# 4-tap convolutions whose running sums stand in the PSUM banks of the scans, with the last tap written to SBUF

## The chip, the cores and the metric

The kernel runs on one core of a Trainium2 chip. The metric is device time in microseconds for one execution. The core has five engines that run at the same time, each through its own list of instructions in order: PE (matrix products), DVE (the vector engine), ACT (the scalar engine, activations), POOL (GpSimd) and SP, which here issues DMAs. They work on SBUF and on PSUM, eight banks of 128 x 512 fp32 that PE writes its products into; DVE and ACT can read and write both. An engine waits where an operand is not there yet, or where the buffer that it is to write is still read.

## The reference, cut to what matters

One layer of a hybrid network over 2048 latent tokens of 1024 values, with 256 context tokens ahead of them. The input projection is split among a Conformer convolution (31 taps), a bidirectional state-space scan (SSD) and a pooling branch; after them come an output projection and a gated MLP with a 3x3 convolution. The change touches the 4-tap convolution ahead of each scan:

```
def _ssd_direction(xbc, dt_raw, conv_w, conv_b, ..., h0, reverse):
    if reverse:
        xbc, dt_raw = xbc[:, ::-1], dt_raw[:, ::-1]
    u = jax.nn.silu(_dwconv1d(xbc, conv_w, conv_b, (SSM_CONV_K - 1, 0)))   # SSM_CONV_K = 4
    xs, Bm, Cm = jnp.split(u, (D_SSM, D_SSM + SSM_GROUPS * SSM_STATE), axis=-1)
    ...
    y, h_final = _ssd_scan(xh, dt, A, Bm, Cm, h0)
```

`xbc` has 1024 channels: 512 of `xs`, 256 of `Bm`, 256 of `Cm`. The convolution runs twice over the same projection with weights of its own, forward in time (direction f) and backward (b). The context runs through the same convolution and scan, without `Cm`, and its last states start the scans of the latent tokens.

## The kernel before, in words

Channels lie on the 128 partitions and tokens along the rows of a tile. The tokens are worked in chunks of 512, of which there are four, 0 to 3. A first sweep runs the context (`ctx_part`), then chunks 0 to 3 forward (`chunk`): projections, both convolutions, the forward scan, the pooling and the 31-tap convolution. A second sweep goes back from chunk 3 with the backward scan and the output projection, and a third part is the MLP. In the profiled execution the first sweep ends at about 716 us.

Every projection (`proj`) of 128 channels by 512 tokens is 24 matmuls: 8 blocks of 128 inputs, each as three products of split values (L114 to L116). It ends in one of four PSUM banks of the pool `mm`. The weights come by DMA from SP (`load_w`), ACT rounds them (L101), POOL subtracts what was rounded off (L102).

In a chunk the eight blocks of `xbc` are projected in the order 4, 5, 6, 7, 0, 1, 2, 3. ACT copies each into a tile `raw` of SBUF (L480; three of them, in turn), with three tokens of the neighbours on either side. `conv4` then forms the forward sum `ca_f` and the backward sum `ca_b`: ACT writes the first tap with the bias (L260), DVE adds three more (L262), ACT applies Silu (L263), forward into `uf` (eight tiles, read by the scan), backward into `ub` (two tiles, sent to DRAM by a DMA and read by the second sweep). The sums stand in three tiles of SBUF, tag `cacc`. They are 512 columns wide forward; backward 509 in chunk 0, 512 in chunks 1 and 2, 515 in chunk 3. In the context both are 256 wide.

The scan works on 128 tokens at a time, in `ssd_in` and `ssd_out`. `ssd_in` forms, in the one bank of the pool `si`, transposes and products (`bps`, `xps`); from there DVE makes `gtm` (L363) and `xde` (L371), and ACT `btm`. `ssd_out` takes three banks in turn from the two of the pool `so`: the state product `st` (L396), which DVE adds to the running state (L399, L402), and the outputs `yo` and `yd`. In the context only `st` is formed, four times: `st_c0_0`, `st_c1_0`, `st_c0_1`, `st_c1_1`, direction first.

In chunk 0 each block is followed by a half of the modulation (`mod_half`): eight weight tiles `wm2` come by DMA and DVE adds them up in a bank `macp` of the pool `lo` (L206, L208), then PE forms `modp` (L211). The pooling sum `pr` (L667) and the 31-tap convolution `c31p` (L585, L588) run on DVE too; `c31p` keeps its sum in a PSUM bank of `lo`, and its last tap goes to SBUF. `dt_path` (L269 and on) computes the step sizes.

The order of the instructions is not that of the code: a scheduler simulates a timeline and lays out each engine's list from it. PSUM and SBUF tiles come from pools that hand out buffers in turn, so a new tile waits until the last reader of the tile that had its buffer is done.

Of the kernel before, what the change touches and what calls it, by code (L numbers as in the profile page):

```python
# [7 lines left out]
F32 = mybir.dt.float32  # L8
F32R = mybir.dt.float32r
AL = mybir.AluOpType  # L10
AF = mybir.ActivationFunctionType
PSUM = bass.MemoryType.PSUM

P = 128
# [34 lines left out]
class Kern:  # L49
# [201 lines left out]

    def conv4(self, out, raw, lo, n, d, j, name):
        nc = self.nc
        acc = self.pc.tile([P, 515], F32, tag="cacc", name=f"ca_{name}", bufs=3)
        base = COFF["sc_w"] + (d * 8 + j) * 4
        for k in range(4):
            off = lo + (k if d == 0 else 3 - k)
            wk = self.cols[:, base + k : base + k + 1]
            if k == 0:
                nc.scalar.activation(acc[:, :n], raw[:, off : off + n], AF.Identity, bias=self.col("sc_b", d * 8 + j), scale=wk)  # L260
            else:
                nc.vector.scalar_tensor_tensor(acc[:, :n], raw[:, off : off + n], wk, acc[:, :n], AL.mult, AL.add)  # L262
        nc.scalar.activation(out, acc[:, :n], AF.Silu)  # L263

    def dt_path(self, hs, n, key, name):
        nc, sp = self.nc, self.sp
# [195 lines left out]
    def chunk(self, c):  # L462
        nc, t, p1 = self.nc, self.t, self.p1
        n = CH
        last = c == NCH - 1
        hs = self.make_h(lambda k: t["xT"][k, :, c * CH : (c + 1) * CH], n, 0, f"c{c}")
        rows = self.dt_path(hs, n, c, f"c{c}")
        for d in range(2):
            nc.sync.dma_start(self.s[f"arow{c}"][d].rearrange("s h l -> (s h) l"), rows[:, d, :])
        self.glu(c, hs)  # L470
        hal = None if last else p1.tile([P, 8, 3], F32, tag="hal", name=f"hal{c}")
        uf = [None] * 8
        for qi, j in enumerate((4, 5, 6, 7, 0, 1, 2, 3)):
            ps = self.proj(self.load_w(t["w_x"][j], f"x{c}_{j}"), hs, n, f"x{c}_{j}")
            raw = self.pc.tile([P, 518], F32, tag="raw", name=f"raw{c}_{j}", bufs=3)
            if c == 0:
                nc.gpsimd.memset(raw[:, 0:3], 0.0)
            else:
                nc.gpsimd.tensor_copy(raw[:, 0:3], self.hal[:, j, :])
            nc.scalar.activation(raw[:, 3:515], ps, AF.Copy)  # L480
            if last:
                nc.gpsimd.memset(raw[:, 515:518], 0.0)
            else:
                nc.gpsimd.tensor_copy(hal[:, j, :], raw[:, 512:515])
            f = self.sp.tile([P, 512], F32, tag="uf", name=f"uf{c}_{j}", bufs=8)
            self.conv4(f, raw, 0, n, 0, j, f"f{c}_{j}")
            uf[j] = f
            b = self.pc.tile([P, 515], F32, tag="ubc", name=f"ub{c}_{j}", bufs=2)
            i0 = 3 if c == 0 else 0
            m = 515 - i0 if last else 512 - i0  # L490
            self.conv4(b[:, :m], raw, i0, m, 1, j, f"b{c}_{j}")
            t0 = c * CH - 3 + i0
            nc.sync.dma_start(self.s["ub"][j, :, t0 : t0 + m], b[:, :m])
            if c == 0:
                self.mod_half(qi)
        self.hal = hal

        def fwd(s):
            nm = f"f{c}_{s}"
            ins[s] = self.ssd_in(0, c, s, uf, s * P, True, nm)  # L500

        def out(s):
            y = self.ssd_out(0, c, s, ins[s], f"f{c}_{s}")
            nc.sync.dma_start(self.s[f"yf{c}"][s * P : (s + 1) * P, :], y)

        ins = {}
        self.ppool(c, hs)
        for s in range(SB - 1):
            fwd(s)
        if not last:  # L510
            self.zproj(c, hs)
        for s in range(NSUB):
            out(s)
            if s + SB - 1 < NSUB:
                fwd(s + SB - 1)
        self.pool_branch(c)
        self.conv_branch(c)
        if last:
            self.zproj(c, hs)
# [538 lines left out]
```

## Time and profile before

| what | value |
|---|---|
| median of 3 runs | 2626.35 us (2623.07 to 2632.42) |
| profiled execution, its own time | 2625.29 us |
| its span, first to last instruction | 2623.6 us |
| mean granted clock of PE | 0.953 |
| busy: PE, DVE, ACT, POOL | 2419.6, 1840.7, 1145.5, 1336.3 us |

Names in the profile are the program's, without their numbers: `ca_f` stands for the forward sums of all chunks, `ps_z` for a projection into `zt`, and so on. A row of a group gives the line, the engine, the operation, what is written and what is read, the count, then the busy time and the mean of one instruction in ns, then how long the engine stood idle just ahead of them and what ended most of it. A row of the timeline gives the start in us, the duration, the instruction, and in brackets how long the engine waited ahead of it and for whom. In the table of stretches stand the borders and the length, then per engine the busy time and the count, then the granted clock, the busy share of the DMA engines and the GB/s that they moved. A row of waits gives the waiting instruction and the one that it waited for, the sum of the waits, their count, the longest.

### The profile page before, as it was taken

What the parts mean: (1) busy time and instruction counts of PE and PEld (TensorE: products, weight loads), DVE (VectorE), ACT (ScalarE), POOL (GpSimd) and SP (SyncE); (2) the same over time, 40 slices, a digit from 0 to 9 for tenths busy, and PEclk for the clock granted to TensorE, in tenths of its full rate; (3) what the DMA queues carried; (4) which work ended last, traced back from release to release, by engine and by line L of the source; (5) the groups of instructions that cost most, each with busy time, mean ns of one, the idle gap of its engine ahead of it and who ended that gap; (6) DMA issues with size and microseconds to landing.
All of it is one profiled execution on the core that took longest, in us unless ns stands there. A gap on an engine that the chain in (4) does not pass through costs nothing.

```text
span 2623.6 us, 31624 instructions
## 1 busy us (share of the span) xinstructions
PE 2419.6 (92%) x11338; PEld 1996.2 (76%) x11338; DVE 1840.7 (70%) x2681; ACT 1145.5 (44%) x1761; POOL 1336.3 (51%) x928
## 2 busy tenths in 40 slices
PE   6897999898777988899999999999999999999996
PEld 3776777677665766689998878888878888788885
DVE  5898978689965776577555497665696664876655
ACT  2656565756553334433334333344333344233342
POOL 2555565554533554544446455455454464454444
PEclk7998999999867999899999999999999999999998
DMA  7655343343335565662224343333343343433332
GB/s 286 202 152 164 110 135 121 117 125 106 123 126 189 185 213 182 194 218 89 89 89 127 100 139 105 96 116 112 114 135 96 97 121 97 152 97 103 99 97 73
DMA packets 125838, 347.01 MB, mean 132 GB/s; under 512 B 19680, under 2 KB 24176, under 8 KB 125680
## 3 DMA queue, kind: packets, MB, share of 16 engines
q1 hardware_dynamic: 121072, 336.60, 40.5%
q10 hardware_dynamic: 4608, 8.39, 1.0%
q8 instruction: 89, 1.46, 0.2%
q14 instruction: 69, 0.57, 0.1%
HBM read 298.63 MB, written 46.31 MB: 131 GB/s over the span
## 4 chain that ended last, share of the span: by engine, by line
PE 59%; DVE 21%; DMA 6%; ACT 6%; issue 4%; POOL 3%; SPq 0%; ACTq 0%; POOLq 0%; DVEq 0%
PE d L114 6%; PE d L116 6%; PE d L115 6%; PE ug L114 5%; PE ug L115 5%; PE ug L116 5%; PE uv L114 5%; PE uv L115 5%; PE uv L116 5%; DVE ca_f L262 2%; DVE ca_b L262 2%; DVE fa L882 1%; DVE c31p L588 1%; ACT E_f L351 1%; DMA wm<-in_w_mod 1%
## 5 line engine op out<-in xcount | busy, mean ns | idle before, releaser
L882 DVE SCALAR_TENSOR_TENSOR fa<-gbuf,cols,fa 128x512 f32<-128x512 f32 x704 | 523.7, 754 | 224.4 <-ACT fa L878 201.8
L912 DVE TENSOR_TENSOR gl<-g,gh 128x512 fp32r<-128x512 f32 x176 | 197.2, 1131 | 217.6 <-ACT gh L911 196.5
L102 POOL TENSOR_TENSOR wl_d<-wr_d,wh_d 128x1024 fp32r<-128x1024 f32 x88 | 222.1, 2525 | 210.6 <-ACT wh_d L101 210.6
L102 POOL TENSOR_TENSOR wl_uv<-wr_uv,wh_uv 128x1024 fp32r<-128x1024 f32 x88 | 220.4, 2504 | 205.9 <-ACT wh_uv L101 205.9
L114 PE MATMUL ug<-h2h,wh_ug 128*128 128x512 f32 (+3 forms) x880 | 309.3, 351 | 17.2 <-DVE g L890 10.6
L102 POOL TENSOR_TENSOR wl_ug<-wr_ug,wh_ug 128x1024 fp32r<-128x1024 f32 x88 | 214.4, 2436 | 192.3 <-ACT wh_ug L101 192.3
L115 PE MATMUL ug<-h2l,wh_ug 128*128 128x512 f32 (+3 forms) x880 | 308.7, 351 | 0.0
L116 PE MATMUL ug<-h2h,wl_ug 128*128 128x512 f32 (+3 forms) x880 | 308.2, 350 | 0.0
L114 PE MATMUL uv<-h2h,wh_uv 128*128 128x512 f32 x704 | 275.6, 391 | 8.8 <-DVE g L890 8.5
L115 PE MATMUL uv<-h2l,wh_uv 128*128 128x512 f32 x704 | 275.3, 391 | 0.0
L116 PE MATMUL uv<-h2h,wl_uv 128*128 128x512 f32 x704 | 274.9, 390 | 0.0
L114 PE MATMUL d<-wh_d,gh 128*128 128x512 f32 x704 | 274.0, 389 | 0.6 <-ACT fg L884 0.4
L115 PE MATMUL d<-wl_d,gh 128*128 128x512 f32 x704 | 273.9, 389 | 0.0
L116 PE MATMUL d<-wh_d,gl 128*128 128x512 f32 x704 | 263.7, 389 | 0.0
L911 ACT ACTIVATE gh<-g 128x512 fp32r<-128x512 f32 x176 | 110.8, 630 | 247.8 <-PE d L115 225.9
L114 PEld LDWEIGHTS ug<-h2h,wh_ug 128*128 128x128 f32 x880 | 168.3, 191 | 37.6 <-DVE g L890 11.9
L101 ACT ACTIVATE wh_ug<-wr_ug 128x1024 fp32r<-128x1024 f32 x88 | 93.2, 1059 | 221.3 <-PE uv L115 188.4
L115 PEld LDWEIGHTS ug<-h2l,wh_ug 128*128 128x128 f32 x880 | 168.2, 191 | 17.8
L116 PEld LDWEIGHTS ug<-h2h,wl_ug 128*128 128x128 f32 x880 | 168.4, 191 | 16.7
L588 DVE SCALAR_TENSOR_TENSOR c31p<-gl,cols,c31p 128x512 f32<-128x512 f32 x232 | 162.1, 749 | 13.6 <-ACT c31p L585 13.4
L114 PEld LDWEIGHTS uv<-h2h,wh_uv 128*128 128x128 f32 x704 | 132.9, 189 | 36.7 <-DVE g L890 9.2
L101 ACT ACTIVATE wh_uv<-wr_uv 128x1024 fp32r<-128x1024 f32 x88 | 93.2, 1059 | 145.5 <-PE ug L115 89.8
(388 smaller groups left out, 5585.5 us busy)
## 6 DMA issues: line engine op xcount, KB each, us to landing
wr_ug<-in_w_up SPq DMA_DIRECT2D x88, 512.0 KB, 3.6
wr_uv<-in_w_up SPq DMA_DIRECT2D x88, 512.0 KB, 3.6
wr_d<-in_w_dn SPq DMA_DIRECT2D x88, 512.0 KB, 3.5
wm<-in_w_mod SPq DMA_DIRECT2D x64, 256.0 KB, 4.0
wr_x<-in_w_x SPq DMA_DIRECT2D x32, 512.0 KB, 3.8
wr_o<-in_w_o SPq DMA_DIRECT2D x32, 512.0 KB, 4.2
wm<-in_w_mod SPq DMA_DIRECT2D x16, 512.0 KB, 8.1
x_c<-in_xT SPq DMA_DIRECT2D x32, 256.0 KB, 3.4
```

Of the source, the lines that this page charges most:

```text
L101: nc.scalar.activation(hi, src, AF.Copy)
L102: nc.gpsimd.tensor_tensor(lo, src, hi.bitcast(F32), AL.subtract)
L114: nc.tensor.matmul(out, a[0], b[0], start=first, stop=False)
L115: nc.tensor.matmul(out, a[0], b[1], start=False, stop=False)
L116: nc.tensor.matmul(out, a[1], b[0], start=False, stop=last)
L262: nc.vector.scalar_tensor_tensor(acc[:, :n], raw[:, off : off + n], wk, acc[:, :n], AL.mult, AL.add)
L351: nc.scalar.activation(E[:, h, :], E[:, h, :], AF.Relu, bias=cum[:, d, s, h : h + 1], scale=-1.0)
L588: nc.vector.scalar_tensor_tensor(to[:, :m], gl[:, j, o + k : o + k + m], w[k], acc[:, :m], AL.mult, AL.add)
L882: nc.vector.scalar_tensor_tensor(acc, G[:, dr : dr + 8, dc : dc + GW], wc[i], acc, AL.mult, AL.add)
L911: nc.scalar.activation(gh, gt[k], AF.Copy)
L912: nc.vector.tensor_tensor(gl, gt[k], gh.bitcast(F32), AL.subtract)
```

## The change

`conv4` takes its running sum from a bank of the pool `so` where the sum has at most 512 columns: all of the context, all forward sums, and the backward sums of chunks 0 to 2. The backward sums of chunk 3, of 515 columns, stay in SBUF, where there are now two tiles `cacc` for three. For all sums the third of DVE's taps no longer goes back into the sum but into `uf` or `ub`, and Silu runs in place there. Silu's line is L267 in the changed kernel, the taps L266, the first tap L263, and later lines move by four.

```
     def conv4(self, out, raw, lo, n, d, j, name):
         nc = self.nc
-        acc = self.pc.tile([P, 515], F32, tag="cacc", name=f"ca_{name}", bufs=3)
+        if n <= 512:
+            acc = self.bank(self.so, f"ca_{name}")
+        else:
+            acc = self.pc.tile([P, 515], F32, tag="cacc", name=f"ca_{name}", bufs=2)
         base = COFF["sc_w"] + (d * 8 + j) * 4
         for k in range(4):
             off = lo + (k if d == 0 else 3 - k)
...
             if k == 0:
                 nc.scalar.activation(acc[:, :n], raw[:, off : off + n], AF.Identity, bias=self.col("sc_b", d * 8 + j), scale=wk)
             else:
-                nc.vector.scalar_tensor_tensor(acc[:, :n], raw[:, off : off + n], wk, acc[:, :n], AL.mult, AL.add)
-        nc.scalar.activation(out, acc[:, :n], AF.Silu)
+                to = out if k == 3 else acc[:, :n]
+                nc.vector.scalar_tensor_tensor(to, raw[:, off : off + n], wk, acc[:, :n], AL.mult, AL.add)
+        nc.scalar.activation(out, out, AF.Silu)
...
-            self.conv4(f, raw, 0, n, 0, j, f"f{c}_{j}")
+            self.conv4(f[:, :n], raw, 0, n, 0, j, f"f{c}_{j}")
```

The scheduler lays out new lists with it. Up to the middle of the second sweep they differ, and from there on the last 7309 rows of PE, 905 of DVE, 824 of ACT, 546 of POOL and 424 of SP stand in the same order as before.

In the rows below a tile's name ends in a number of its own, and x2 or x4 counts equal rows. The first place is DVE where chunk 0's convolutions begin. Before, `state_c0_0`, the first copy of a context state, was followed by the taps of block 4, and the operands `xde` of the other three states came between taps:

```order
L208 SCALAR_TENSOR_TENSOR macc4_1410<-wm2_4_7_1432,scol_138,macp4_1409 128x512
L399 COPY state_c0_0_707<-st_c0_0_704 128x512
L262 SCALAR_TENSOR_TENSOR ca_f0_4_1067<-raw0_4_1062,cols_105,ca_f0_4_1067 128x512
L262 SCALAR_TENSOR_TENSOR ca_b0_4_1074<-raw0_4_1062,cols_105,ca_b0_4_1074 128x509
L262 SCALAR_TENSOR_TENSOR ca_f0_4_1067<-raw0_4_1062,cols_105,ca_f0_4_1067 128x512
L262 SCALAR_TENSOR_TENSOR ca_b0_4_1074<-raw0_4_1062,cols_105,ca_b0_4_1074 128x509
L262 SCALAR_TENSOR_TENSOR ca_f0_4_1067<-raw0_4_1062,cols_105,ca_f0_4_1067 128x512
L371 TENSOR_TENSOR xde_c1_0_719<-xps_c1_0_714,ex_ctx_686 128x512
L262 SCALAR_TENSOR_TENSOR ca_b0_4_1074<-raw0_4_1062,cols_105,ca_b0_4_1074 128x509
```

Now all four states' operands stand ahead of the first tap, and the last addition, `state_c1_1`, ahead of the first backward tap:

```order
L403 COPY state_c0_0_707<-st_c0_0_704 128x512
L375 TENSOR_TENSOR xde_c1_0_719<-xps_c1_0_714,ex_ctx_686 128x512
L403 COPY state_c1_0_724<-st_c1_0_721 128x512
L375 TENSOR_TENSOR xde_c0_1_736<-xps_c0_1_731,ex_ctx_686 128x512
L406 TENSOR_TENSOR state_c0_1_741<-state_c0_1_741,st_c0_1_738 128x512
L375 TENSOR_TENSOR xde_c1_1_754<-xps_c1_1_749,ex_ctx_686 128x512
L266 SCALAR_TENSOR_TENSOR ca_f0_4_1067<-raw0_4_1062,cols_105,ca_f0_4_1067 128x512 x2
L212 TENSOR_TENSOR modc2_115<-modp5_1517,cols_105 128x4
L266 SCALAR_TENSOR_TENSOR uf0_4_1066<-raw0_4_1062,cols_105,ca_f0_4_1067 128x512
...
L208 SCALAR_TENSOR_TENSOR macp6_1573<-wm2_6_1_1578,scol_138,macp6_1573 128x512
L406 TENSOR_TENSOR state_c1_1_759<-state_c1_1_759,st_c1_1_756 128x512
L266 SCALAR_TENSOR_TENSOR ca_b0_4_1074<-raw0_4_1062,cols_105,ca_b0_4_1074 128x509
```

So the first forward tap moved behind `xde_c1_1`, and the backward taps of the same block, which alternated with it, behind the end of the context's scan.

The second place is PE at the fourth context state. Before, the matmul `st_c1_1` and the transposes `dtT` of chunk 0 stood between the whole projections of blocks 2 and 3:

```order
L114 MATMUL ps_x0_2_1529<-hhi_c0_7_813,wh_x0_2_1524 128x512
L115 MATMUL ps_x0_2_1529<-hlo_c0_7_814,wh_x0_2_1524 128x512
L116 MATMUL ps_x0_2_1529<-hhi_c0_7_813,wl_x0_2_1525 128x512
L396 MATMUL st_c1_1_756<-xde_c1_1_754,btm_c1_1_747 128x256 x2
L275 MATMUL dtT_c0_845<-ident_107,dtr_c0_843 128x40 x4
L114 MATMUL ps_x0_3_1611<-hhi_c0_0_764,wh_x0_3_1606 128x512
L115 MATMUL ps_x0_3_1611<-hlo_c0_0_765,wh_x0_3_1606 128x512
L116 MATMUL ps_x0_3_1611<-hhi_c0_0_764,wl_x0_3_1607 128x512
```

Now they stand in the projection of block 2, behind its first three matmuls:

```order
L116 MATMUL ps_x0_1_1447<-hhi_c0_7_813,wl_x0_1_1443 128x512
L211 MATMUL modp5_1517<-ones_122,macc5_1492 128x2 x4
L114 MATMUL ps_x0_2_1529<-hhi_c0_0_764,wh_x0_2_1524 128x512
L115 MATMUL ps_x0_2_1529<-hlo_c0_0_765,wh_x0_2_1524 128x512
L116 MATMUL ps_x0_2_1529<-hhi_c0_0_764,wl_x0_2_1525 128x512
L400 MATMUL st_c1_1_756<-xde_c1_1_754,btm_c1_1_747 128x256 x2
L279 MATMUL dtT_c0_845<-ident_107,dtr_c0_843 128x40 x4
L114 MATMUL ps_x0_2_1529<-hhi_c0_1_771,wh_x0_2_1524 128x512
L115 MATMUL ps_x0_2_1529<-hlo_c0_1_772,wh_x0_2_1524 128x512
L116 MATMUL ps_x0_2_1529<-hhi_c0_1_771,wl_x0_2_1525 128x512
```

The state matmul moved forward by the 21 other matmuls of that projection.

The third place is ACT where the raw tiles of chunk 0's first blocks are filled and emptied (`wh` rows are weights that ACT rounds). Before, `raw0_7` was copied behind Silu of the second block's backward sum, `ub0_5`:

```order
L480 ACTIVATE raw0_6_1226<-ps_x0_6_1201 128x512
L260 ACTIVATE ca_f0_6_1231<-raw0_6_1226,cols_105 128x512
L260 ACTIVATE ca_b0_6_1238<-raw0_6_1226,cols_105 128x509
L263 ACTIVATE ub0_5_1155<-ca_b0_5_1156 128x509
L101 ACTIVATE wh_x0_2_1524<-wr_x0_2_1523 128x1024
L480 ACTIVATE raw0_7_1308<-ps_x0_7_1283 128x512
L263 ACTIVATE ub0_6_1237<-ca_b0_6_1238 128x509
```

Now it stands behind the first tap of that sum, `ca_b0_5`, whose bank `ca_b0_4` has to leave first:

```order
L267 ACTIVATE uf0_4_1066<-uf0_4_1066 128x512
L263 ACTIVATE ca_b0_4_1074<-raw0_4_1062,cols_105 128x509
L263 ACTIVATE ca_f0_5_1149<-raw0_5_1144,cols_105 128x512
L293 ACTIVATE dt_e_c0_851<-dt_x_c0_850 128x64
L294 ACT_TABLE_LOAD
L294 ACTIVATE dt_e_c0_851<-dt_e_c0_851 128x64
L101 ACTIVATE wh_p0_1_1720<-wr_p0_1_1719 128x1024
L267 ACT_TABLE_LOAD
L267 ACTIVATE ub0_4_1073<-ub0_4_1073 128x509
L263 ACTIVATE ca_b0_5_1156<-raw0_5_1144,cols_105 128x509
L484 ACTIVATE raw0_7_1308<-ps_x0_7_1283 128x512
L267 ACTIVATE uf0_5_1148<-uf0_5_1148 128x512
```

The Silus of block 5 and the first taps of block 6, which stood ahead of it, now come behind it, and the loads of activation tables (`ACT_TABLE_LOAD`) fall between other rows; there are 49 of them in the whole program where there were 45.

## The prediction

> **What bounds the kernel now.** I read the page first: the busy line of each engine, the slices of the span, the chain of work that ended last. Then the stretches of the first third, because only there the changed lines run, then what PE waited for in them, and last single rows on DVE and POOL where PE waited longest.
>
> ```profile
> PE 2419.6 (92%) x11338; PEld 1996.2 (76%) x11338; DVE 1840.7 (70%) x2681; ACT 1145.5 (44%) x1761; POOL 1336.3 (51%) x928
> PE 59%; DVE 21%; DMA 6%; ACT 6%; issue 4%; POOL 3%; SPq 0%; ACTq 0%; POOLq 0%; DVEq 0%
> ...
> L262 DVE SCALAR_TENSOR_TENSOR ca_f<-raw,cols,ca_f x96: 644/745/2900, 130.1 to 669.6; 128x512 f32<-128x512 f32 x96
> ```
>
> PE is the bound of the program as a whole. The taps of the 4-tap convolutions, L262, are done before 680 us, and behind the first sweep, which ends at about 716 us, nothing of the changed code runs; there I forecast no difference. So the question is how much PE idles in the first 716 us, and for whom. In these stretches (borders at the starts of the chunks' convolutions) the columns are the stretch and its length, then busy time and count for PE, PEld, DVE, ACT, POOL, and the granted clock:
>
> ```profile
> 90.00:230.00 140.00, 122.98 (x547) 97.47 (x545) 122.47 (x185) 80.94 (x129) 71.79 (x55) 0.93 0.54 170
> 230.00:291.00 61.00, 55.73 (x280) 44.70 (x281) 54.04 (x84) 36.32 (x61) 33.76 (x24) 0.97 0.46 139
> 291.00:442.00 151.00, 140.63 (x654) 110.76 (x653) 122.54 (x189) 96.68 (x155) 87.46 (x66) 0.97 0.39 126
> 442.00:601.00 159.00, 143.07 (x681) 113.31 (x679) 127.91 (x199) 95.90 (x156) 86.65 (x67) 0.98 0.39 118
> 601.00:716.00 115.00, 97.25 (x422) 75.84 (x421) 112.33 (x199) 68.19 (x117) 60.30 (x39) 0.91 0.34 113
> ```
>
> PE idles 17.0, 5.3, 10.4, 15.9 and 17.8 us in them. Up to 601 us it is PE's own work with DVE a close second (77 to 89% busy); from 601 to 716 us DVE is busy 112.33 of 115 us, so the end of the sweep hangs on DVE.
>
> **What the taps cost.** A tap that keeps its sum in SBUF takes 745 ns at the median, yet its mean is far higher. Taps of the 31-tap convolution, L588, of the same shape, keep their sum in PSUM:
>
> ```profile
> L588 DVE SCALAR_TENSOR_TENSOR c31p<-gl,cols,c31p 128x512 f32<-128x512 f32 x232 | 162.1, 749 | 13.6 <-ACT c31p L585 13.4
> L262 DVE SCALAR_TENSOR_TENSOR ca_f<-raw,cols,ca_f 128x512 f32<-128x512 f32 x96 | 96.7, 1008 | 31.1 <-ACT ca_f L260 30.8
> L262 DVE SCALAR_TENSOR_TENSOR ca_b<-raw,cols,ca_b 128x512 f32<-128x512 f32 x48 | 43.0, 896 | 0.1
> L262 DVE SCALAR_TENSOR_TENSOR ca_b<-raw,cols,ca_b 128x509 f32<-128x509 f32 x24 | 28.3, 1178 | 0.0
> L262 DVE SCALAR_TENSOR_TENSOR ca_b<-raw,cols,ca_b 128x515 f32<-128x515 f32 x24 | 22.8, 950 | 2.2 <-ACT ca_b L260 2.1
> ...
> L588 DVE SCALAR_TENSOR_TENSOR c31p<-gl,cols,c31p x232: 733/749/760, 217.3 to 740.0; 128x512 f32<-128x512 f32 x116
> L588 DVE SCALAR_TENSOR_TENSOR c<-gl,cols,c31p x8: 734/738/748, 288.4 to 740.8; 128x512 f32<-128x512 f32 x8
> ...
> 508.41 2.88 DVE L262 SCALAR_TENSOR_TENSOR ca_f<-raw,cols,ca_f 128x512 f32<-128x512 f32 x1
> ...
> 507.93 2.81 POOL L102 TENSOR_TENSOR wl_z<-wr_z,wh_z 128x1024 fp32r<-128x1024 f32 x1 [1.39 <-ACT wh_z L101]
> ```
>
> The last two rows show one long tap: it begins 0.48 us into a POOL subtraction and ends 0.55 us behind its end. None of the 232 PSUM taps exceeds 760 ns, though POOL works half of the time. So I take it that only the tap with both inputs in SBUF waits for POOL. The last tap of the 31-tap convolution reads SBUF and PSUM and writes SBUF, as the new last tap does, and takes 738 ns: no wait either.
>
> **The change, part by part.** DVE: 72 + 24 + 24 + 24 = 168 taps of chunks 0 to 3 in direction f and chunks 0 to 2 in b go to PSUM (x96 of ca_f, x48 and x24 of ca_b); the 24 of 515 columns stay in SBUF. Saved: 96 x (1008 - 749) + 48 x (896 - 749) + 24 x (1178 - 749) = 24.9 + 7.1 + 10.3 = 42 us of DVE's time, and some 8 us more on 36 taps of the context, before 108 us, where input DMAs and the modulation set the pace; those I count at nothing. Of the 42 us most lies beside PE's work. By stretch (DVE's busy time and count first; ca_f and ca_b apart in chunk 0, L262 as a whole in chunks 1 and 2, ca_f alone in chunk 3; a PSUM tap's own share, with the overlap of rows taken off, is 162.1 / 232 = 0.70 us):
>
> ```profile
> 90.00:230.00 140.00, 23.01 (x24) 11.32 (x16) 0.93 0.54 170
> 90.00:230.00 140.00, 28.27 (x24) 11.17 (x16) 0.93 0.54 170
> 291.00:442.00 151.00, 47.43 (x49) 0.97 0.39 126
> 442.00:601.00 159.00, 41.47 (x48) 0.98 0.39 118
> 601.00:716.00 115.00, 23.56 (x24) 10.41 (x15) 0.91 0.34 113
> ```
>
> Above 0.70 us a tap this is 17.7 us in chunk 0, 13 in chunk 1, 8 in chunk 2 and 6.8 (f alone) in chunk 3. What of it PE waited for between 230 and 601 us:
>
> ```profile
> PE xps_f L369 <- DVE gtm_f L363: 10.9, 3, 7.5
> ...
> 518.08 1.11 PE L369 MATMUL xps_f<-ident,uf 128*128 128x128 f32 x4 [7.54 <-DVE gtm_f L363]
> 518.84 0.77 PE L116 MATMUL ps_z<-hhi_c,wl_z 128*128 128x512 f32 x1
> ...
> 522.36 0.39 PE L115 MATMUL ps_z<-hlo_c,wh_z 128*128 128x512 f32 x1
> ...
> 526.94 0.39 PE L114 MATMUL ps_z<-hhi_c,wh_z 128*128 128x512 f32 x1
> ```
>
> (a) Chunks 1 and 2. `gtm_f` stands on DVE right behind a chunk's convolutions and holds the bank that PE wants; 7.5 us in chunk 2 and, of the other 3.4 us (10.9 - 7.5), 2.6 us in chunk 1 are the convolutions' lateness. It will not all go: ahead of `gtm_f` stand two `pr` rows of the pooling that wait for POOL,
>
> ```profile
> 512.65 0.73 DVE L667 SCALAR_TENSOR_TENSOR pr<-ps,cols,pb 64x512 f32<-64x512 f32 x1
> 514.63 2.93 DVE L667 SCALAR_TENSOR_TENSOR pr<-ps,cols,pb 64x512 f32<-64x512 f32 x1 [1.24 <-POOL ps L646]
> ```
>
> and POOL itself was late, since its subtraction waits for ACT, whose Silu waits for the taps. I take 6 of the 7.5 us as gone, plus 1.7 us of slow matmuls behind the gap (8 steps of 0.44 us from 518.84 to 522.36, then 20 of 0.23 us: 8 x 0.21), and chunk 1's 2.6 us with 0.4 us of the same: 8 + 3 = 11 us. Bounds: 0, if `pr` alone sets `gtm_f`; 17 us, if the 15 us of both rows go, with 2 us of slow matmuls.
>
> (b) Chunk 3 and the end of the sweep. DVE is the limit there, so DVE time saved is time saved: 6 us (the 6.8 above, less rows that wait for other engines). Bounds 2, if half the lateness returns as waits for ACT, and 10, the 6.8 and DVE's own 2.7 us of idling.
>
> (c) Chunk 0. The two PSUM banks are those of the scans, in turn. The context's four state matmuls come between its convolutions and chunk 0's, so the first tap, at 130.1 us before, must now wait for the third state, and the backward one for the fourth (159.5 and 176.2 us before):
>
> ```profile
> 130.12 0.75 DVE L262 SCALAR_TENSOR_TENSOR ca_f<-raw,cols,ca_f 128x512 f32<-128x512 f32 x1 [2.40 <-ACT ca_f L260]
> 159.53 0.67 DVE L402 TENSOR_TENSOR state_c<-state_c,st_c 128x512 f32<-128x512 f32 x1
> 176.23 0.68 DVE L402 TENSOR_TENSOR state_c<-state_c,st_c 128x512 f32<-128x512 f32 x1
> 168.29 2.07 PE L396 MATMUL st_c<-xde_c,btm_c 128*128 128x256 f32 x4 [2.98 <-DVE xde_c L371]
> 203.53 0.98 PE L211 MATMUL modp<-ones,macc 128*128 128x2 f32 x4 [4.95 <-DVE macc L208]
> 207.26 0.64 PE L314 MATMUL cum_c<-dt_a_c,tri 128*128 128x32 f32 x2 [2.75 <-DVE dt_a_c L309]
> ```
>
> The new order draws the fourth state matmul 21 matmuls forward (5 us at 0.23 us) and takes its operand's row, which PE awaited for 3.0 us, ahead of the taps; so I set the last state at 176 - 5 - 3 = 168 us at the latest, and at about 161 us if PE runs there without the waits it had from 138 us on. From 161 us: ACT's first tap 0.8, the three backward taps of j = 4 with six rows of other work between them, 9 x 0.75 = 6.8, then ACT's Silu, next first tap and copy, 2.0 us: at about 171 us a raw tile and a PSUM bank come free for PE's projection of x3. It ran from about 171 us before too, behind the state matmul of 168.29 us and four transposes. Further on DVE owes 17.7 us less of locks and one modulation half less (8 rows of some 0.75 us, 6 us, drawn ahead of the taps), against the 26 us from 130 to 156 us in which it has no tap. So PE's 4.95 and 2.75 us at 203 to 207 us may shrink, and new waits for raw tiles may come (three tiles, each held until its backward sum is written). I take 0; bounds: -8 us, both waits gone, and +22 us, worked out with rival 2.
>
> (d) The rest:
>
> ```profile
> L263 ACT ACT_TABLE_LOAD x13 | 16.7, 1283 | 0.2
> L263 ACT ACTIVATE ub<-ca_b 128x512 f32<-128x512 f32 x16 | 10.0, 627 | 7.8 <-DVE ca_b L262 7.7
> L260 ACT ACTIVATE ca_f<-raw,cols 128x512 f32<-128x512 f32 x32 | 25.9, 809 | 0.8
> L585 ACT ACTIVATE c31p<-gl,cols 128x512 f32<-128x512 f32 x8 | 6.0, 772 | 0.0
> 139.28 1.54 DVE L262 SCALAR_TENSOR_TENSOR ca_f<-raw,cols,ca_f 128x512 f32<-128x512 f32 x2 [0.21 <-ACT ca_f L260]
> ```
>
> The last tap now waits on DVE for the tile that it writes, where Silu waited on ACT; Silu's waits were all for taps, none for a DMA that empties the tile, so I price this at nothing. If the cover went, each late DMA would stop DVE, and with it ACT's next first tap. ACT's first tap takes 772 ns into PSUM for 809 ns: 56 x 0.04 = 2 us on ACT, hidden beside DVE's taps. Two taps of one sum behind each other take 1.54 us, 0.1 us more than two of 0.70 us; the new order has 9 more such pairs, 1 us of DVE, hidden in (b)'s rounding. The new order has 49 table loads on ACT for 45, two more in chunk 0 and two in chunk 3: 4 x 1.3 = 5 us, for which I charge nothing, since ACT works 81 of 140 us in the one and 68 of 115 us in the other; without that cover each would hold a Silu, and behind it the taps of a later sum, by 1.3 us, so chunk 3's 2.6 us are within (b)'s lower bound. Silu runs in place on SBUF as it read SBUF before; the third SBUF sum buffer goes, and only chunk 3's backward sums use the two that are left.
>
> Sum: -11 - 6 + 0 = -17 us. The profiled execution took 2625.3 us (span 2623.6), 1.1 us under the median of 2626.35. So 2608 us on its scale, 2609 us for the median.
>
> [...]
>
> **Rivals.** (1) The taps were hidden anyway: PE is 92% busy, `pr` and POOL keep `gtm_f` late, and only the end of the sweep gains. For it speaks POOL's wait row above; against it that POOL itself hung on the taps by way of ACT. Time: 2626 - 6 = 2620 us. (2) Slower: chunk 0's late convolutions. If the fourth state stays at 176 us, chunk 0's pairs of convolutions start 46 us later than 130.1 us; less 17.7 us of locks and 6 us of modulation done ahead, DVE is 22 us late, and PE, with three raw tiles and four banks, loses as much. With (a) and (b) that is 2626 + 22 - 17 = 2631 us, with (b) alone 2642 us; I set it at 2636 us. It decides from a fourth state at about 170 us on, where the 24 us of relief no longer cover the delay. Against it speaks that PE's order has that matmul three rows into the projection of x2, which began 24 rows ahead of 168.29 us. (3) Larger gain: chunk 0 also loses its 8 us of waits, and (a) comes near its bound: 2626 - 30 = 2596 us.
>
> **Numbers.** Forecast 0.55, rival 1 0.23, rival 2 0.14, rival 3 0.08. A difference of 0.3% is 7.9 us. Faster than 2618.5 us are the forecast but for a small part, and rival 3: 0.62. Rival 1 and a rest are within 0.3%: 0.23. Slower 0.15. The range leaves out most of rival 2 and the far half of rival 3: 2596 to 2630 us; the forecast's own is 2600 to 2618 us.
>
> **What would show it.** No tap in PSUM above 760 ns, group means near 749 ns, and long rows only among the 515-column ones. PE's wait for `gtm_f` in chunk 2 below 2 us. The last forward state matmul of the sweep about 17 us earlier, the stretch from 811 us on as long as before. The fourth context state at about 161 us, the projection x3 of chunk 0 starting at about 171 us. Wrong it would be if DVE's saved time turns into waits for ACT, whose first tap now needs a bank that the tap two sums earlier must have left, or if chunk 0's PE waits exceed 15 us.

## The result, and the profile after

The changed kernel takes 2609.3 us (median of 4 runs, 2605.0 to 2611.4), the kernel before, run beside it, 2624.9 us. The ratio is 0.9934, 95% interval 0.9918 to 0.9951: 0.66% faster, 16 us. The forecast was 2609 us. The total came out as forecast; two of the terms of its sum did not, and they cancelled, which was luck.

The profiled execution took 2605.0 us, 4.3 us under its median; its span is 2603.3 us, 20.3 us shorter than that of before. The busy line of the page:

```profile
PE 2403.8 (92%) x11338; PEld 1987.1 (76%) x11338; DVE 1791.9 (69%) x2681; ACT 1149.7 (44%) x1765; POOL 1303.9 (50%) x928
```

DVE is busy 49 us less, where the working had 42 us and 8 us of the context. The taps, one row for each form, with minimum, median and maximum in ns and the starts of the first and the last:

```profile
L266 DVE SCALAR_TENSOR_TENSOR ca_f<-raw,cols,ca_f x64: 734/748/756, 154.9 to 649.0; 128x512 f32<-128x512 f32 x64
L266 DVE SCALAR_TENSOR_TENSOR ca_b<-raw,cols,ca_b x64: 734/748/2045, 162.0 to 651.0; 128x512 f32<-128x512 f32 x32, 128x509 f32<-128x509 f32 x16, 128x515 f32<-128x515 f32 x16
L266 DVE SCALAR_TENSOR_TENSOR uf<-raw,cols,ca_f x32: 644/736/748, 158.0 to 653.0; 128x512 f32<-128x512 f32 x32
L266 DVE SCALAR_TENSOR_TENSOR ub<-raw,cols,ca_b x32: 720/742/755, 166.2 to 655.8; 128x512 f32<-128x512 f32 x16, 128x509 f32<-128x509 f32 x8, 128x515 f32<-128x515 f32 x8
```

The forward taps, all in PSUM, reach 756 ns at most, where the same rows in SBUF reached 2900 ns. Only the backward group still has long ones (up to 2045 ns); it holds the sums of 515 columns, which stayed in SBUF.

Where the time went is read from the start of the same matmul, counted by its name, in the traces. The points are the first projection into a raw tile of chunks 1, 2 and 3, the last forward state matmul `st_f`, the first matmul of the output projection `o`, the first of the MLP `ug` and the last of all, `d`. E1 is the first experiment below.

| start in us | chunk 1 | chunk 2 | chunk 3 | last st_f | first o | first ug | last d |
|---|---|---|---|---|---|---|---|
| before | 280.5 | 433.8 | 584.6 | 727.2 | 811.0 | 1116.0 | 2602.2 |
| after | 272.4 | 420.4 | 563.4 | 705.5 | 785.9 | 1095.8 | 2581.9 |
| after less before | -8.1 | -13.4 | -21.2 | -21.7 | -25.1 | -20.2 | -20.3 |
| E1 less before | +1.5 | +5.2 | +4.3 | +5.9 | -0.8 | +6.4 | +5.8 |

So context and chunk 0 gave 8.1 us, chunks 1 and 2 together 13.1, chunk 3 with the end of the sweep 0.5. Behind it 3.4 us were won up to the output projection, 4.9 lost up to the MLP, and nothing changed in the MLP. Two cautions go with such a table. Each column is one execution: that of E5 below, whose lists are the changed kernel's until well into chunk 3, reaches chunk 3 2.8 us later, so differences of up to 3 us say little. And the lists differ in how many of PE's matmuls stand ahead of chunk 1's first projection, 1056 before and 1050 after; behind 1056 matmuls the changed kernel leads by 6.7 us, and chunks 1 and 2 then give 14.5. From chunk 2 on the counts are equal.

The stretches, with the columns of the same table of before and the same borders, though the changed kernel's work lies up to 22 us earlier in them:

```profile
90.00:230.00 140.00, 123.23 (x559) 96.96 (x558) 96.22 (x182) 87.95 (x136) 66.74 (x59) 0.94 0.54 172
230.00:291.00 61.00, 60.11 (x307) 48.44 (x306) 54.87 (x86) 33.23 (x60) 34.45 (x27) 0.99 0.45 140
291.00:442.00 151.00, 142.14 (x689) 114.50 (x688) 121.69 (x215) 102.00 (x164) 80.67 (x68) 0.99 0.41 130
442.00:601.00 159.00, 150.04 (x708) 119.11 (x707) 128.99 (x226) 100.38 (x161) 82.93 (x68) 0.99 0.39 121
601.00:716.00 115.00, 89.44 (x388) 70.09 (x386) 105.56 (x171) 65.05 (x114) 50.40 (x36) 0.84 0.41 130
```

From 90 to 230 us DVE is 26 us less busy, and PE's idle time hardly moves (16.8 us for 17.0), though more matmuls are done there (559 for 547). From 230 to 601 us PE idles 18.7 us where it idled 31.6.

### The profile page after: what moved, and what is told of

Read it like the earlier page. It is cut to its first block, busy times and chain, and to the rows that moved or that the text cites. A ratio compares the mean times of both kernels' runs of the same rounds, so it can differ in the third digit from the quotient of the medians.

```text
span 2603.3 us, 31634 instructions
## 1 busy us (share of the span) xinstructions
PE 2403.8 (92%) x11338; PEld 1987.1 (76%) x11338; DVE 1791.9 (69%) x2681; ACT 1149.7 (44%) x1765; POOL 1303.9 (50%) x928
## 4 chain that ended last, share of the span: by engine, by line
PE 61%; DVE 20%; DMA 6%; ACT 6%; issue 3%; POOL 2%; SPq 0%; ACTq 0%; DVEq 0%; POOLq 0%
PE d L114 6%; PE d L116 6%; PE d L115 6%; PE ug L114 5%; PE ug L115 5%; PE ug L116 5%; PE uv L114 5%; PE uv L115 5%; PE uv L116 5%; DVE c31p L592 2%; DVE fa L886 1%; DVE xt L783 1%; ACT E_f L355 1%; DMA x_c<-in_xT 1%; PE o L114 1%
## 5 line engine op out<-in xcount | busy, mean ns | idle before, releaser
L116 PEld LDWEIGHTS ug<-h2h,wl_ug 128*128 128x128 f32 x880 | 168.6, 192 | 16.8
L592 DVE SCALAR_TENSOR_TENSOR c31p<-gl,cols,c31p 128x512 f32<-128x512 f32 x232 | 162.2, 746 | 20.3 <-ACT c31p L589 20.0
```

Source lines behind the costliest of these rows:

```text
L116: nc.tensor.matmul(out, a[1], b[0], start=False, stop=last)
L592: nc.vector.scalar_tensor_tensor(to[:, :m], gl[:, j, o + k : o + k + m], w[k], acc[:, :m], AL.mult, AL.add)
```

## The experiments

Theory: taps with both inputs in SBUF waited for POOL's subtraction, and the PSUM sums only take these waits away. Rivals: the new order of the lists brought the gain, or the last tap's place did. Several kernels are held to the order of another: the program is built twice, and the second build's instructions get order-only edges along the first one's lists, engine by engine (shortened, as are the other cuts of code):

```
first = build_one(arrays, "psum")               # the kernel whose order is wanted
...
for n in first.order:                           # n: place of an instruction in the code
    i = mine[n]
    if i.engine in last:
        tc.add_manual_dep(i, last[i.engine].name, NoSync, ...)
    last[i.engine] = i
```

**E1: the changed kernel's order, sums in SBUF.**

```
-        if n <= 512:
+        if n <= 512 and self.mode == "psum":
             acc = self.bank(self.so, f"ca_{name}")
         else:
-            acc = self.pc.tile([P, 515], F32, tag="cacc", name=f"ca_{name}", bufs=2)
+            w, tag = (512, "cacf") if n <= 512 else (515, "cacc")
+            acc = self.pc.tile([P, w], F32, tag=tag, name=f"ca_{name}", bufs=2)
```

> The changed kernel with every engine's list in exactly the changed kernel's order, but the running sums in two SBUF tiles of their own in place of the two PSUM banks; the last tap still goes to uf or ub, Silu is still in place. Theory (waits for POOL): the taps' mean goes back from 745 ns to 950 ns or more, DVE's busy time before 716 us grows by about 40 us, and the time goes back to within 6 us of the kernel before, that is 10 to 20 us above the changed kernel. Rival (the new order or the last tap's place brought the gain): the taps are long again, but the time stays within 4 us of the changed kernel.

Measured: 2630.3 us, ratio to before 1.0010 (0.9998 to 1.0023), span 2629.3 us. The groups of its taps:

```profile
L267 DVE SCALAR_TENSOR_TENSOR ca_f<-raw,cols,ca_f 128x512 f32<-128x512 f32 x64 | 59.8, 934 | 19.6 <-ACT ca_f L264 19.4
L267 DVE SCALAR_TENSOR_TENSOR ca_b<-raw,cols,ca_b 128x512 f32<-128x512 f32 (+2 forms) x64 | 57.2, 894 | 8.0 <-ACT ca_b L264 7.7
L267 DVE SCALAR_TENSOR_TENSOR uf<-raw,cols,ca_f 128x512 f32<-128x512 f32 x32 | 37.9, 1183 | 0.2
L267 DVE SCALAR_TENSOR_TENSOR ub<-raw,cols,ca_b 128x512 f32<-128x512 f32 (+2 forms) x32 | 30.0, 938 | 0.2
```

The theory holds and the first rival falls: with every list in the same order the whole gain is gone. This splits the change in two. At one order the faster taps are worth 21 us by the medians (2630.3 to 2609.3) and 26 us by the two spans (2629.3 to 2603.3); the changed kernel's profiled execution was the fastest of its four. The new order with sums in SBUF is 5.8 us behind the kernel before in the table, but its ratio to it has 1 within the interval, so a cost of the order by itself is not shown.

**E2: DVE's first tap reads SBUF twice and writes the bank.**

```
+            one = self.pc.tile([P, 512], F32, tag="cacf", ...)     # ACT's first tap goes here
...
-    nc.vector.scalar_tensor_tensor(to, raw[...], wk, acc[:, :n], AL.mult, AL.add)
+    nc.vector.scalar_tensor_tensor(to, raw[...], wk, (one if k == 1 else acc)[:, :n], AL.mult, AL.add)
```

> The changed kernel, same order on every engine, but ACT's first tap goes to an SBUF tile, so DVE's first tap reads two SBUF tiles and writes the PSUM bank; the other two are as in the changed kernel. Theory (a tap waits for POOL when both inputs are in SBUF, wherever it writes): a third of the 168 taps is long again, mean of that third above 0.95 us with single ones above 2.5 us, the other two thirds stay below 760 ns, and the time rises by a third of what the sums in SBUF cost, 3 to 7 us above the changed kernel. Rival (only a tap that also writes SBUF waits): no tap above 760 ns and the time as the changed kernel's within 3 us.

Measured: 2613.5 us, ratio 0.9946 (0.9928 to 0.9965), 4.2 us above the changed kernel's median, with intervals that overlap; it is the rows that decide. Forward taps by form, those that read `cs_f` in SBUF first:

```profile
L267 DVE SCALAR_TENSOR_TENSOR ca_f<-raw,cols,cs_f x32: 740/755/1808, 155.1 to 650.5; 128x512 f32<-128x512 f32 x32
L267 DVE SCALAR_TENSOR_TENSOR ca_f<-raw,cols,ca_f x32: 736/750/756, 155.9 to 653.7; 128x512 f32<-128x512 f32 x32
L267 DVE SCALAR_TENSOR_TENSOR uf<-raw,cols,ca_f x32: 649/739/750, 158.1 to 657.7; 128x512 f32<-128x512 f32 x32
```

Two inputs in SBUF make a tap long although it writes PSUM (up to 1808 ns); with one input in PSUM it is not (756 ns at most), although it writes SBUF (`uf`, 750 ns at most). The size was off: the means of the first taps in the chunks are 820 ns forward and 842 ns backward, not above 950, and none exceeds 2.1 us.

**E3: the kernel before, its own order, without POOL's subtraction in the first sweep.** POOL fills the low halves of these weights with zeros instead, so this kernel leaves them out of its products.

```
-        self.split(w, hi, lo)
+        if self.mode == "fill" and name[0] in "xcgapz":  # weights of the context and the chunks
+            self.nc.scalar.activation(hi, w, AF.Copy)
+            self.nc.gpsimd.memset(lo.bitcast(F32), 0.0)
+        else:
+            self.split(w, hi, lo)
```

> The kernel before, every engine's list in its own order, but POOL's subtraction for the weights of the context and of the four chunks is a memset of the same tile (the low halves of these weights are left out of the products). Theory (POOL's two-input subtraction is what the SBUF taps wait for): the mean of the SBUF taps falls from 980 to 1008 ns to below 800 ns without any PSUM sum, DVE's busy time before 716 us falls by 30 us or more, and the time falls by 8 to 20 us. Rival (the taps are slow for another reason, their own SBUF traffic or the DMAs'): the taps stay above 950 ns and the time within 4 us of the kernel before. If a memset holds DVE as well, long taps stay, but as long as a memset's rest.

Measured: 2551.4 us, ratio 0.9712 (0.9697 to 0.9726). The groups, then one tap on DVE's timeline and the memset on POOL's that it lies in:

```profile
L266 DVE SCALAR_TENSOR_TENSOR ca_b<-raw,cols,ca_b 128x512 f32<-128x512 f32 (+2 forms) x96 | 74.7, 778 | 2.4 <-ACT ca_b L264 2.1
L266 DVE SCALAR_TENSOR_TENSOR ca_f<-raw,cols,ca_f 128x512 f32<-128x512 f32 x96 | 73.8, 769 | 44.7 <-ACT ca_f L264 42.1 <-POOL hal L488 2.3
```

```profile
142.36 0.75 DVE L266 SCALAR_TENSOR_TENSOR ca_b<-raw,cols,ca_b 128x509 f32<-128x509 f32 x1
141.95 0.95 POOL L111 MEMSET wl_x<- 128x1024 f32 x1 [3.13 <-PE ps_x L120]
```

The SBUF taps fall to 769 and 778 ns without any sum in PSUM, and a memset does not hold the tap that starts within it (0.75 us). So POOL's two-input subtraction is the cause of the long taps. The gain of 76 us is far above the 8 to 20 us expected: the taps are one of several groups of DVE that this subtraction holds (the twelve `pr` rows of 512 columns fall from 927 to 744 ns on average; of the 85 us by which DVE's busy time falls, 1840.7 to 1755.8 us, the taps of the chunks give 42), and POOL itself needs 0.95 us for 2.6 us. How much of it is whose was not separated.

**E4: the last tap back in the bank, Silu reads the bank.** `to = acc[:, :n]` for all taps, and `activation(out, acc[:, :n], AF.Silu)`.

> The changed kernel, same order on every engine, but the last tap goes back into the PSUM bank and Silu reads the bank and writes uf or ub. Theory (the banks alone carry the gain): last taps of 749 ns for 737 ns, 56 x 12 ns = 0.7 us of DVE, Silu a little slower, the time within 3 us of the changed kernel. Rival (the last tap's place matters, since it frees a bank one ACT instruction earlier): the banks come free 0.6 us or more later for each of 56 sums, ACT's first taps wait, and the time rises by 5 us or more.

Measured: 2610.8 us, ratio 0.9942 (0.9925 to 0.9959), span 2605.0 us for 2603.3. The second rival falls: the last tap's place can't be told from nothing.

**E5: ACT's list at the end of the sweep.** In the changed kernel this is what stands around DVE's longest wait in chunk 3 (DVE's, ACT's and PE's rows of its timeline):

```profile
641.77 3.13 DVE L592 SCALAR_TENSOR_TENSOR c31p<-gl,cols,c31p 128x512 f32<-128x512 f32 x4 [7.43 <-ACT c31p L589]
646.24 0.76 DVE L266 SCALAR_TENSOR_TENSOR ca_f<-raw,cols,ca_f 128x512 f32<-128x512 f32 x1 [1.34 <-ACT ca_f L263]
...
634.81 1.28 ACT L356 ACT_TABLE_LOAD   x1
636.11 1.06 ACT L356 ACTIVATE E_f<-E_f 128x1024 f32<-128x1024 f32 x1
637.07 1.04 ACT L101 ACTIVATE wh_z<-wr_z 128x1024 fp32r<-128x1024 f32 x1
638.13 1.28 ACT L267 ACT_TABLE_LOAD   x1
...
639.96 0.58 ACT L484 ACTIVATE raw<-ps_x 128x512 f32<-128x512 f32 x1
...
640.96 0.77 ACT L589 ACTIVATE c31p<-gl,cols 128x512 f32<-128x512 f32 x1
...
645.59 0.79 PE L114 MATMUL ps_z<-hhi_c,wh_z 128*128 128x512 f32 x1 [4.52 <-ACT pb L544]
```

ACT stands idle nowhere here. The first tap of `c31p` comes behind an exponential, a rounding and two table loads, and DVE waits 7.43 us for it; before, with slower taps, DVE's longest wait in chunk 3 was 2.1 us. The faster taps did not bring this wait, though: E1, with the same lists and slow taps, has it as well:

```profile
DVE c31p L593 <- ACT c31p L590: 7.0, 1, 7.0
```

```
act = [n for n in order if n is an instruction of ACT]
# rows 564 to 597: raw, c31p, pb and the first taps ahead of the two E_f groups
new = [564, 573, 582, 584, 586, 588, 585, 587, 591, 592, 593, 565..572, 594, 595, 590, 583, 574..581, 589, 596, 597]
```

> The changed kernel with the lists of all engines in its own order, except 34 rows of ACT at the end of the first sweep: the copy of the last raw tile, the first taps of the 31-tap convolution and of the last 4-tap sums and the copies into pb come ahead of the two E_f groups (16 Relus and 2 exponentials), which now stand behind them. In the changed kernel DVE idles 7.4 us there ahead of c31p and 1.3 us ahead of ca_f, both for ACT, and PE 4.5 us for pb. Theory (ACT's list took back what the faster taps gave in chunk 3): these waits fall below 2 us each, the last forward states come 4 to 7 us sooner and the time is 3 to 7 us below the changed kernel's. Rival (the end of the sweep hangs on PE's or POOL's late work anyway): the waits appear elsewhere and the time stays within 2 us.

Measured: 2603.2 us, 6.1 us below the changed kernel's median, ratio 0.9919 (0.9896 to 0.9943), whose interval overlaps the changed kernel's. The last `st_f` starts at 705.7 us (changed kernel: 705.5), but this execution had reached chunk 3 2.8 us later, so the stretch from there is 2.6 us shorter (139.5 for 142.1 us). DVE's timeline of this kernel:

```profile
638.27 3.12 DVE L592 SCALAR_TENSOR_TENSOR c31p<-gl,cols,c31p 128x512 f32<-128x512 f32 x4
...
645.26 2.90 DVE L266 SCALAR_TENSOR_TENSOR ca_b<-raw,cols,ca_b 128x515 f32<-128x515 f32 x1
649.12 0.16 DVE L670 TENSOR_TENSOR ps<-ps,pedge 64x8 f32<-64x8 f32 x1 [0.96 <-POOL ps L650]
...
652.62 0.42 DVE L367 TENSOR_TENSOR gtm_f<-bps_f,tri 128x256 f32<-128x256 f32 x1 [2.01 <-ACT btm_f L364]
```

The wait of 7.43 us is gone and DVE is 5.7 us further at 649 us, but a 515-column tap in SBUF takes 2.90 us where another takes 0.75 (at 642.62 us; that POOL held the long one is inferred), and DVE waits for POOL's `ps` and for `btm`, which now stands late on ACT. At 656 us 0.6 us of the lead is left. Over the stretch DVE's waits fall from 8.7 to 3.0 us, and its busy time rises from 132.9 to 136.1 us. So ACT's rows did hold chunk 3, and moving them brings the next waits and long rows: the outcome lies between the theory (4 to 7 us sooner) and the rival, and the time does not decide.

**E6, E7: the low halves stored.** Chunk 0 writes its 18 low halves to DRAM, chunks 1 to 3 read them; on the changed kernel (E6) and on the kernel before (E7).

```
+        if chunk 0:
             self.split(w, hi, lo)
+            self.nc.sync.dma_start(self.s[f"wlow{i}"], lo.bitcast(F32))
+        else:
+            self.nc.scalar.activation(hi, w, AF.Copy)
+            self.nc.sync.dma_start(lo.bitcast(F32), self.s[f"wlow{i}"])
```

> The changed kernel, but chunk 0 also writes the low halves of its weights (18 blocks of 0.5 MB) to DRAM, and chunks 1 to 3 read them from there by DMA in place of POOL's subtraction; the scheduler lays out new lists. Theory (POOL's subtraction holds more of DVE's rows than the taps): without it in three of four chunks the stretch from 244 us on gains most of the 48 us that the kernel before with a memset gained there, less the 11 us that the PSUM sums already have: 20 to 35 us below the changed kernel. Rival (the 27 MB more of reads and 9 MB of writes make weights late): less than 8 us below, or slower, with new waits of PE for wl by DMA.

> The same on the kernel before, with its sums in SBUF. Theory (both edits take away the same waits): 30 to 45 us below the kernel before, and the distance to the changed kernel with the same edit shrinks from 16 us to the 9 us of chunk 0 and a few more, 6 to 13 us. Rival (the PSUM sums help by something else than POOL's waits): the distance stays at 16 us or more.

Measured: E6 2569.5 us, ratio 0.9784 (0.9762 to 0.9806); E7 2582.8 us, ratio 0.9837 (0.9816 to 0.9858). E6 is 40 us below the changed kernel, above the 20 to 35 us expected; the rival's late weights do not show, as none of PE's waits from 263 to 720 us in E6 is for a DMA. The distance of the two, 13.3 us, lies at the edge of what was expected. Chunk 1's first projection (263.1 us in E6, 279.9 in E7) is not the place to measure it, since 1056 matmuls stand ahead of it in E6 and 1088 in E7. Behind 1104 matmuls E7 is 12.0 us late (283.7 for 271.7), at chunk 2 14.0 (416.9 for 402.9), at the last `st_f` 15.6 (680.8 for 665.2). So nearly all of it is made up to chunk 1; over chunks 2 and 3, where POOL no longer subtracts, sums in PSUM bring 1.6 us, too little to tell from nothing.

**E8: the changed kernel, its own order, POOL's subtraction replaced as in E3.**

> The changed kernel, every list in its own order, but POOL's subtraction for the weights of the context and of the four chunks is a memset of the same tile (their low halves are left out of the products), as it was tried on the kernel before. Theory (the PSUM sums bring only what POOL's subtraction cost the taps): the two kernels without it differ only by their order, 0 to 12 us, the changed one not faster: 2550 to 2563 us. Rival (the PSUM sums bring a gain of their own): the changed one stays 10 us or more below the other, at about 2535 us.

Measured: 2571.1 us, ratio 0.9793 (0.9771 to 0.9816), 20 us slower than E3. The sign is the theory's, the size is not: 0 to 12 us were expected. Chunk 1 starts at 266.7 us (E3: 252.9) and from there to the last `st_f` it takes 408.4 us (E3: 399.2). Without the subtraction (the means of the taps `ca_f` and `ca_b` are 752 and 751 ns here, 769 and 778 in E3) the changed kernel is the worse one; whether by its order or by the two banks that its sums share with the scans, this does not separate.

**E9: chunk 0's first block in SBUF.** `if n <= 512 and name not in ("f0_4", "b0_4")`.

> The changed kernel, but the two sums of chunk 0's first block (4) stand in the two SBUF tiles that only chunk 3 uses otherwise, so that they need no bank of the scans; the scheduler lays out new lists. Theory (the context's states hold chunk 0's convolutions back, and that is what the new order costs): the first tap starts at about 130 us instead of 155 us, PE's waits at 169 us (4.1 us) and from 204 to 228 us (10 us in all) shrink, the projections after 244 us run 3 to 9 us sooner than in the changed kernel, less up to 3 us for six taps that wait for POOL again: time 2 to 8 us below. Rival (chunk 0's later blocks wait for the banks and for POOL just the same): the stretch to 244 us stays within 2 us.

Measured: 2608.3 us, ratio 0.9928 (0.9911 to 0.9945): no gain to be told from nothing. The first taps do start early (126.3 us for 154.9 in the changed kernel), and the first two take 1.47 and 1.52 us where the next four take 0.73 to 0.74 (that POOL held them is inferred):

```profile
126.26 1.47 DVE L266 SCALAR_TENSOR_TENSOR ca_f<-raw,cols,ca_f 128x512 f32<-128x512 f32 x1 [1.35 <-ACT ca_f L263]
127.65 1.52 DVE L266 SCALAR_TENSOR_TENSOR ca_b<-raw,cols,ca_b 128x509 f32<-128x509 f32 x1
```

Chunk 1 starts 3.6 us sooner than in the changed kernel (268.8 us) and the last `st_f` 5.9 us sooner (699.6), as the theory had it. The MLP starts 6.8 us later (1102.6). The lists differ in the second sweep too, and there all of it is lost in this execution; why was not tried.

**E10, E11, E12: both halves stored.** E10 writes both halves in chunk 0 and reads both in chunks 1 to 3, E11 is E10 with E9's block in SBUF, E12 writes the low halves in chunk 0 and the high ones in chunk 1.

> The changed kernel with both halves of the weights written to DRAM in chunk 0 and read in chunks 1 to 3, so that POOL's subtraction and ACT's rounding both fall away there. Theory (ACT's list holds DVE at the end of the sweep, and 54 roundings of 1.06 us are its largest part): PE's waits for pb and ya and DVE's for c31p shrink, 5 to 15 us below the kernel that stores the low halves alone (2569 us). Rival (18 MB of writes in chunk 0 make its own loads late): chunk 0 loses 5 us or more, and the time stays at 2569 us or above.

> The same with the two sums of chunk 0's block 4 in SBUF. If both theories hold their gains add: 2 to 8 us below the kernel with both halves stored.

> As the kernel with both halves stored, but the high halves are written in chunk 1, where the DMA engines are less busy (46 to 39% instead of 54%), and read in chunks 2 and 3; the low halves are written in chunk 0 as before. In the kernel with both written in chunk 0 the DMA engines were 92% busy from 90 to 230 us and the stretch to 255 us ended 13 us later than with the low halves alone, and chunk 1 made that good by some 12 us. Theory (writes in chunk 0 cost what ACT's relief gives): chunk 0 ends as with the low halves alone, about 19 us ahead of the kernel before, chunks 2 and 3 gain as with both halves, and the time is 3 to 10 us below 2563.7 us. Rival (PE is already 98 to 99% busy from 291 to 601 us, so there is nothing left to gain there): within 3 us of it.

Measured: E10 2563.7 us, ratio 0.9759 (0.9745 to 0.9774); E11 ratio 0.9749 (0.9732 to 0.9765), not to be told from E10, so the 2 to 8 us expected of it are not shown; E12 2556.3 us, ratio 0.9739 (0.9716 to 0.9761), span 2552.5 for E10's 2563.3. By the medians E10 is 5.8 us below E6 and E12 7.4 us below E10, as their theories had it, but each of these pairs of intervals overlaps. The stretch of chunk 0 in E10, and in E12, with the DMA engines' share and their GB/s at the end:

```profile
90.00:230.00 140.00, 133.12 (x638) 106.44 (x637) 115.38 (x202) 87.94 (x144) 68.23 (x60) 0.98 0.92 326
```

```profile
90.00:230.00 140.00, 130.51 (x623) 103.50 (x623) 108.75 (x192) 93.21 (x146) 67.75 (x61) 0.96 0.79 274
```

Chunk 1 starts at 270.4 us in E10, 261.3 us in E12 (E6: 263.1), but behind 1104, 1076 and 1056 matmuls. Behind 1104 in each, E10 stands at 270.4 us, E12 at 267.2, E6 at 271.7, and chunk 2 starts at 403.7, 402.8 and 402.9 us. So E10's writes in chunk 0 do not show as a loss against E6, although the DMA engines are 92% busy there; at an equal count the 13 us in E12's expectation are not seen. What the stored high halves give is seen in chunk 3, from its first projection to the last `st_f`: 127.3 us in E6, 121.7 in E10, 121.9 in E12. E12's lead over E10 is 1.4 us at that `st_f` and 9.3 at the first `o`; why it grows there was not tried. Its theory met the number, not by the path that it named. E11 starts chunk 2 7.6 us later than E10 (411.3), so E9's early start did not add up with the stored halves.

E12 has the lowest time of the kernels that leave nothing out of the products: 70 us below the kernel before, 53 below the changed one.

## Why the prediction was right, point by point

**What bounds, and the taps.** Right: the 42 us and 8 us of DVE's waits were there to be had and went. (The 168 taps are 96 + 48 + 24; "72 + 24 + 24 + 24" makes 144, but the saving was worked out with the right counts.) E1 to E3 show the cause that was inferred from two rows. Against it the `pr` rows, which still read SBUF twice, take 20.8 us for 16.8 before; E1 has 20.4, so that comes with the order.

**(a) Chunks 1 and 2.** Forecast -11, measured -13.1. PE's waits from 230 to 601 us in the changed kernel:

```profile
PE xps_f L373 <- DVE gtm_f L367: 5.3, 3, 4.2
PE pw L634 <- ACT ya L636: 4.9, 2, 3.6
```

The 7.5 us in chunk 2 are gone. In chunk 1 the wait for `gtm_f` grew from 2.6 to 4.2 us, and `pw`'s for ACT, in both chunks together, from 4.3 to 4.9 us. By the table the taps at one order gave 15.9 us; the 2.8 us that the order took back are within what two executions of one order differ by.

**(b) Chunk 3 and the end of the sweep.** Forecast -6, bounds -2 and -10; measured -0.5. From chunk 3's first projection to the last `st_f`, in us:

| kernel | length | DVE busy | DVE's waits |
|---|---|---|---|
| before | 142.6 | 139.8 | 2.1 |
| after | 142.1 | 132.9 | 8.7 |
| E1 | 144.2 | 135.4 | 8.4 |
| E5 | 139.5 | 136.1 | 3.0 |

In all four DVE's busy time and its waits add up to the stretch, less 0.4 to 0.7 us, so "DVE is the limit there" holds. Its busy time fell by 6.9 us, the 6.8 that were worked out. The step that failed is "so DVE time saved is time saved": its waits grew by 6.6 us, all for ACT. The lower bound named such waits as the taps' lateness that returns, but E1 has them with slow taps. They come with the new order of ACT's list, for which the sum charged nothing, since ACT works 68 of 115 us there. That is an average: from 635 to 645 us ACT has no gap, and table loads, priced at nothing too, stand among its rows there. At one order the taps gave 2.1 us.

**(c) Chunk 0.** Forecast 0, bounds -8 and +22; measured -8.1 with the context. The picture of its pieces was right. The last addition to the context's states, and the projection of x3:

```profile
161.03 0.67 DVE L406 TENSOR_TENSOR state_c<-state_c,st_c 128x512 f32<-128x512 f32 x1
```

```profile
169.03 0.50 PE L114 MATMUL ps_x<-hhi_c,wh_x 128*128 128x512 f32 x1 [4.09 <-ACT raw L484]
```

They were set at about 161 and 171 us. The late start costs little by itself: in E1, with slow taps, the first matmul of `ps_z` in chunk 0 starts at 198.9 us, 9.1 us later than before, but 6.1 us of this stand there already at chunk 0's first projection (119.6 us for 113.5). With sums in PSUM neither place moves (113.8 and 189.7 us for 113.5 and 189.8). What was sized too low is the relief behind it. The modulation, drawn ahead of the taps, ends 27 us earlier (the last start in each row; before, then after):

```profile
L211 PE MATMUL modp<-ones,macc x64: 165/251/353, 47.1 to 227.9; 128*128 128x2 f32 x64
```

```profile
L211 PE MATMUL modp<-ones,macc x64: 165/251/352, 48.9 to 201.3; 128*128 128x2 f32 x64
```

So PE's 4.95 and 2.75 us at 203 to 207 us went; other waits came, but from the first `ps_z` matmul to the 1056th of all they add up to 11.1 us for 14.4 before, and the stretch takes 84.1 us for 90.7. E1 has the same, 84.5 us with 11.4 us of waits: the gain of chunk 0 comes from the order, not from faster taps. What the taps gave at one order, 9.6 us up to chunk 1, kept the new order from costing about as much ahead of that stretch: 5.8 us in the context (113.8 us after, 119.6 in E1) and 3.4 from there to `ps_z`. Against the kernel before, the context changed by 0.3 us, so pricing it at nothing came true.

**(d) The rest.** Forecast 0. The last tap's place is worth nothing measurable (E4). That "the stretch from 811 us on" stays as long as before was wrong: from the first `o` on, the changed kernel takes 4.9 us longer to the MLP, and E1, with the same order, 7.2 us. So it does not come from the taps. Counted from the last `st_f`, with 1545 matmuls in each, the way to the MLP takes 388.7 us before, 390.3 after and 389.3 in E1: what is lost behind the first `o` had mostly been won ahead of it.

**The rivals.** The hidden taps (2620 us) had it the wrong way round: only the end of the sweep was to gain, and it is the one stretch that did not. The slower outcome did not come; the fourth state stood at 161 us, on the safe side of the 170 us that were named. The larger gain had the size of chunk 0 about right and both waits gone, though others took part of their place. Of the signs of being wrong one came: in chunk 3 saved DVE time stood against new waits for ACT.

## What to carry to other kernels

A group whose mean lies far above its median (here 1008 to 745 ns) may wait inside its instructions, where no list of waits names it. Look for the instruction of another engine that ends just ahead of the long one, and ask what the two share; here one operand in another memory took 21 us away at one order, and keeping what the other engines had worked out again in each chunk took 53 us more. An engine that is 98% busy in a stretch, as DVE was in chunk 3, can be its limit and its saved time still come to nothing, when it then waits longer for an engine that it alternates with: read that engine's new list before booking the time. A change that makes a scheduler lay out a new order is two changes; holding the order fixed tells them apart. And where two lists differ, compare them behind the same number of matmuls: the start of a named row moved by up to 48 matmuls here.

## What the hardware showed that was not expected

POOL loses time as well. Its subtraction for the raw projections, before and after:

```profile
L102 POOL TENSOR_TENSOR wl_x<-wr_x,wh_x 128x1024 fp32r<-128x1024 f32 x32 | 84.3, 2634 | 55.9 <-ACT wh_x L101 54.9 <-DVE c31p L588 1.0
```

```profile
L102 POOL TENSOR_TENSOR wl_x<-wr_x,wh_x 128x1024 fp32r<-128x1024 f32 x32 | 77.4, 2420 | 78.2 <-ACT wh_x L101 72.4 <-DMA wr_x<-in_w_x 3.4 <-PE ps_x L116 1.3
```

It is 214 ns shorter where the taps read PSUM. At one order it is 147 ns (2567 ns in E1, with sums in SBUF), and there the forward taps in `ca_f` take 934 ns for 748: so each of the two engines sometimes waited for the other.
